# Layer 0's S5 scratch in a pool below the filter's, and the S5 phase doublings on VectorE

## The chip, the cores and the metric

One core of a Trainium2 chip runs the whole program in one launch. The metric is device time in microseconds, the median of several runs. Engines: PE is TensorE (matrix products), DVE is VectorE, ACT is ScalarE, POOL is GpSimd, SP issues the DMA transfers. Each engine works through its own queue in order; semaphores tie the queues together.

## The reference

The model is a two-layer block on 256 latent tokens and 256 context tokens of width 1024. Each layer does the following:

```
h = modulate(rmsnorm(x), shift, scale)      # shift, scale from silu(c) @ ada_w + ada_b
p = h @ w_in                                # columns: Fourier 256, hyena 1152, S5 384
y = concat(fourier(p_f), hyena(p_h, filter), s5(p_s)) @ w_out
x = x + gate * y
x = x + gate_f * ffn(modulate(rmsnorm(x)))  # layer 0: SwiGLU; layer 1: top-2 of 8 experts
```

The hyena filter is a small sine network over 256 positions, windowed, normalised and taken to the frequency domain. It depends on weights only. S5 is a diagonal complex state space, in 24 groups of 16 channels and 64 states, scanned in both directions. Its transition per step is exp(lambda dt), a decay times a phase. The kernel scans over chunks of 8 tokens and turns the states by tables of phases, cos and sin of multiples of the angle, so that the scan itself is real. The multiples come from doublings: squaring a unit complex number and pulling its length back to one.

## The kernel before

The program is written with a tile framework. Tiles are taken from pools, pools lie on two stacks of the on-chip memory (left and right, growing towards each other), and a pool that is closed gives its room to the next one opened on that side. A tile on room that had an owner waits until the owner's pool is released, that is until every access to it has ended. A planner orders each engine's queue at build time from the data dependences, the order in which the program is written (earlier has priority) and its own costs; it also puts waits where memory is reused. So the order on an engine isn't the order of the text.

The start of layer 0, in the order of the text: the pool `filt` (left) holds the filter network `hy_filter` (constants, `hfb`, `hs`, `hd`, `ab`, `rk`, `Kf`). Above it lie `prm` (the S5 parameters, `s5_params`) and `start` (the input `xin`, the norm's scratch, weight tiles). `hy_filter` first runs up to its two sines; then the modulation rows (`ada_pe`), the norm `norm_h` (squares, `rsqrt_small`, then for each of 8 column blocks `nf`, `hH` and `hL`, with `hL` on GpSimd for even blocks and on VectorE for odd ones, L500), then `s5_params`, then the rest of `hy_filter`: for each of two orders the products `pf`, their windowing `hfb` on VectorE, sums `hs` and differences `hd` on GpSimd (L754, L755), and the products `pk`, which become `Kf` and are stored to DRAM (`kd<-Kf`, L772).

`s5_params` computes on 128 x 48 tiles, all on VectorE, up to cos and sin of the angle (`cs`, `sn`). Nine doublings follow (the loop over k), all on GpSimd: `cmul` squares (L241 to L246) from k=1 on, then L360 to L365 normalise. The last six results (`gen`) feed the tables `rotB` and `rotA`, 36 products on GpSimd.

Then `filt` is closed, and `mixers(0, ...)` runs in the pools `z0p` (left, where `filt` was: `uf`, `z0`, `x1`, `x2` and, under one tag, `U` and `ysT`) and `ada0`. On the right it opens `s5p0` (X and the scans' scratch), three matrix buffers `M2`, `M1`, `M0` and, as the last and lowest of that stack, `scr`, the scratch of `s5_mats`. The projection's blocks 11 to 13 are the S5 input: projected (`pacc`), evacuated (`u`, L994), transposed (`pU`, L997), written to `U` (L999), gathered by products into `X` (L1007). `mats(q)` builds the matrices of one sixth of the groups: loads `bs`, `cs` and `d16`, forms `bb`, `bre`, `bim`, writes `M` and clears and fills `rh`, sends `R` to DRAM and reads it back into M (`M<-rd`). `s5_sixth(q)` runs the sixth: products `pv`, two scans on VectorE, the states `Sre`, `Sim`, products `py`. Between sixths, `hy_tile` projects and filters hyena blocks into `z0`, `x1`, `x2`, and `fill0` makes further modulation rows (`ada_ring`). At q=4 `scr` and `M0` are closed and the convolution `conv` of the hyena begins; its products on VectorE use `t_a` (two buffers) and `t_b` (one), each for two of the four products.

After layer 0's mixers come its output projection and feed-forward, with the modulation rows of `ada` (tiles `ar`, `jk` on VectorE, `pd` on GpSimd; the last two in the lasting pool `par`).

Of the kernel before, what the change touches and what calls it, by code (L numbers as in the profile page):

```python
# [8 lines left out]
F32 = mybir.dt.float32  # L9
F32R = mybir.dt.float32r  # L10
I32 = mybir.dt.int32
# [5 lines left out]
D = 1024  # L17
# [5 lines left out]
HY = 384  # L23
S5G = 24
# [109 lines left out]
def build(tc, A, out, dbg=None, upto='all'):  # L134
# [3 lines left out]
    gtt = G.tensor_tensor  # L138
# [109 lines left out]
    def s5_params(p, s5p):  # L248
# [100 lines left out]
        pr, pi = cs, sn  # L349
        t1, t2 = T("gt1"), T("gt2")  # L350
        gen = p.tile([128, 6, 2, 48], F32, name="gen")
        for k in range(9):
            if k >= 3:
                d_re, d_im = gen[:, k - 3, 0], gen[:, k - 3, 1]
            else:
                d_re, d_im = T(f"ph{k}r"), T(f"ph{k}i")
            q_re, q_im = (pr, pi) if k == 0 else (T(f"q{k}r"), T(f"q{k}i"))
            if k:
                cmul(q_re, q_im, pr, pi, pr, pi, t1, t2, G)
            gtt(t1, q_re, q_re, op=mul)  # L360
            gtt(t2, q_im, q_im, op=mul)
            gtt(t1, t1, t2, op=add)
            G.tensor_scalar(t1, t1, -0.5, 1.5, op0=mul, op1=add)
            gtt(d_re, q_re, t1, op=mul)
            gtt(d_im, q_im, t1, op=mul)  # L365
            pr, pi = d_re, d_im
        u, v = (p.tile([128, 48, 4], F32, name=n) for n in ("rtu", "rtv"))
        for tab, k0 in ((rotB, 0), (rotA, 3)):
# [58 lines left out]
    def ada(l, m0, m1, eng, pool):  # L427
        for m in range(m0, m1):
            r = pool.tile([128, D], F32, name="ar", tag="ar", bufs=2)
            SP.dma_start(r, A['adaT'][l, m])  # L430
            for s in range(1 if l == 1 and m >= 16 else 0, 2):
                o = mods[l][:, m, s:s + 1]
                if eng(m, s) == 'v':
                    jk = par.tile([128, D], mybir.dt.bfloat16, name="jk", tag="jk", bufs=1)
                    stt(jk, r, 1.0, crow[:, s], op0=mul, op1=mul, accum_out=o)
                else:
                    pd = par.tile([128, D], F32, name="pd", tag="pd", bufs=1)
                    gtt(pd, r, crow[:, s], op=mul)  # L438
                    act(pd, pd, AF.Copy, accum_out=o)  # L439
            if m % 8 == 7:  # L440
                mods_done(l, m - 7, 8, 1 if l == 1 and m >= 16 else 0)
# [258 lines left out]
    def hy_filter(p, l, kd):  # L700
# [10 lines left out]
                                ap=[[0, 128], [HY, 2], [1, HY]]))  # L711

        def sine(src, b, fr, nm):
            a = p.tile([64, 256], F32, name=nm + "a", tag="sina")
            i = p.tile([64, 256], I32, name=nm + "i", tag="sini")
            nf = p.tile([64, 256], F32, name=nm + "n", tag="sinn")
            o_ = p.tile([64, 256], F32, name=nm + "o", tag="sino", bufs=2)
            ts_(a, src, b, fr, op0=add, op1=mul)
            ts_(i, a, INV2PI, None, op0=mul)
            V.tensor_copy(nf, i)  # L720
            stt(a, nf, -6.28125, a, op0=mul, op1=add)
            stt(a, nf, -1.9350051879882812e-3, a, op0=mul, op1=add)
            stt(a, nf, -3.0199159819567529e-7, a, op0=mul, op1=add)
            ts_(a, a, -3.1415925, 3.1415925, op0=OP.max, op1=OP.min)
            act(o_, a, AF.Sin)
            return o_
# [45 lines left out]
                SP.dma_start(kd[:, o_, f], K)  # L772


    def mixers(l, hH, hL, z2, yH, yL, fill):
        t0 = 0 if l == 0 else 256
        n = 512 - t0
        ns = n // 256
# [76 lines left out]
        def conv(p, K, src0, src1):  # L855
            ce = Kt[1]
            pu = []
            for f in range(4):
                pf = pt_('h' if f < 2 else 'h2', (128, HY), "pU")
                mm(pf, ce[:, f // 2, (f % 2) * 128:(f % 2) * 128 + 128], src0 if f < 2 else src1, True, True)  # L860
                pu.append(pf)
            Yf = p.tile([128, 4, HY], F32, name="Yf", bufs=ns)
            for f in range(2):
                ta, tb, tc_, td = (p.tile([128, HY], F32, name=n_, tag=n_, bufs=b_) for n_, b_ in
                                   (("t_a", 2), ("t_b", 1), ("t_a", 2), ("t_b", 1)))
                tt_(ta, pu[f], K[:, f], op=mul)
                tt_(tb, pu[2 + f], K[:, 2 + f], op=mul)
                gtt(Yf[:, f], ta, tb, op=sub)
                tt_(tc_, pu[f], K[:, 2 + f], op=mul)
                tt_(td, pu[2 + f], K[:, f], op=mul)  # L870
                gtt(Yf[:, 2 + f], tc_, td, op=add)
            return Yf
# [98 lines left out]
        with tc.tile_pool(name=f"s5p{l}", bufs=1, side="right") as p, banks(mat=2, s5=2):  # L971
# [2 lines left out]
            mes, mpool = [ExitStack() for _ in range(nm)], [None] * nm  # L974
            for i in range(nm - 1, -1, -1):
                mpool[i] = mes[i].enter_context(tc.tile_pool(name=f"M{i}_{l}", bufs=1, side="right"))
            SC = ExitStack()
            if l == 0:
                scr = SC.enter_context(tc.tile_pool(name="scr", bufs=1, side="right"))

            U = z2.tile([128, S5G, 4, 16], F32, name="U", tag="ysT")
            raws = {}
            pas = {}
            if l:
# [16 lines left out]
            for q in range(3):  # L1001
# [3 lines left out]
                        mm(px[64 * (1 - par):128 - 64 * par, g], U[:, 8 * q + g].rearrange("p j h -> p (j h)"),  # L1005
                           sel[:, par], True, True)
                act(X[:, 8 * q:8 * q + 8], px, AF.Copy)  # L1007
            ysT = z2.tile([128, 3, n], F32, name="ysT", tag="ysT")
            order = HYO[l]
            done = 0  # L1010

# [19 lines left out]
            for th in range(3):  # L1031
                Y = p.tile([128, 4 if l == 0 else 2, 128], F32, name="Y")
                for h in range(2):
                    q = 2 * th + h
                    if q + nm <= 6 and len(ms) < q + nm:
                        ms.append(mats(q + nm - 1))
                    if l == 0 and q == 4:
                        SC.close()
                        mes[0].close()
                        hA = hes.enter_context(tc.tile_pool(name="hyA0", bufs=1))  # L1040
                        hcon(hA)
                    s5_sixth(p, l, q, *ms[q], X, Y)
                    for _ in range((NHY0, NHY)[l][q]):
                        hy_tile(order[done], raws)
                        done += 1
                    fill(q)
                    if q == (4, 2)[l]:
                        Y0 = [conv(hA, Kt[0], z0[:, s, 0], z0[:, s, 1]) for s in range(ns)]
                    if l and q == 4:
                        zz = hy_second(hp, Y0)  # L1050
                    if l and q == 5:
                        fourier(hp, *fo)
                        hy_last(hp, zz)
                s5_out(l, th, Y, ysT)
# [23 lines left out]
    mdr = [dr.tile([128, 4, 768], F32, name=f"md{q}") for q in range(6)]  # L1078
    rhdr = [dr.tile([128, 4, 64], F32, name=f"rh{q}") for q in range(6)]
    rdr = [dr.tile([32, 4, 240], F32, name=f"rd1{q}") for q in range(6)]  # L1080
    z_es = ExitStack()
    with tc.tile_pool(name="filt", bufs=1) as p_:
        th = tmp.tile([128, KD, 2], F32, name="sth", tag="sth", bufs=1)
        act(th, scol, AF.Tanh, scale=0.5)
# [29 lines left out]
    with z_es:  # L1114
# [3 lines left out]
        with tc.tile_pool(name="z0p", bufs=1) as z2, tc.tile_pool(name="ada0", bufs=1) as p_:  # L1118
            def fill0(q):
                if q == 0:  # L1120
                    ada_ring(4, p_)
                if q == 1:
                    ada_ring(5, p_)
                if q == 3:
                    ada_ring(6, p_)
                if q == 4:
                    ada_ring(7, p_)
            mixers(0, hH, hL, z2, yH, yL, fill0)
        tap('yH0', yH.bitcast(F32))
        tap('yL0', yL.bitcast(F32))  # L1130
        rx_es, xp = ExitStack(), ExitStack()
# [686 lines left out]
```

## Time and profile before

| | |
|---|---|
| median of 3 runs | 1852.7 us (1851.32 to 1853.93) |
| profiled execution | 1846.75 us, of which the span 1844.9 |
| PE busy | 1708.1 us (93%) |
| DVE busy | 824.4 us (45%) |
| ACT busy | 445.1 us (24%) |
| POOL busy | 535.0 us (29%) |
| mean granted PE clock | 0.964 |

The span runs from the first to the last instruction. Busy times of engines overlap, so they don't add up to it. Matrix products are pipelined, and a busy PE isn't PE at its peak. [...] Roughly the second half of the span is layer 1's experts.

### The profile page before, as it was taken

The page shows a single profiled execution, that of the slowest core. Times are in us where ns is not written, and L with a number is a line of the kernel's source. Part 1 is how long each engine was busy: PE and PEld are TensorE (multiplying, and loading weights), DVE is VectorE, ACT ScalarE, POOL GpSimd, SP SyncE. Part 2 cuts the span into 40 slices and gives each one's busy share as a digit, 9 for nine tenths or more (in the row PEclk, how much of TensorE's full clock was granted, in tenths as well). Part 3 has the DMA queues.
Part 4 walks back from the last instruction along what each step waited for, and adds up shares of the span by engine and source line. Part 5 has one row for each costly group of instructions (what it writes and reads, how often), then busy time and mean ns, then how long its engine had stood idle before and what let it go on. Part 6 is the DMA issues. An engine that isn't in the chain of part 4 may idle for free. (4 is left out here: it accounts for less than half of the span.)

```text
span 1844.9 us, 47520 instructions
## 1 busy us (share of the span) xinstructions
PE 1708.1 (93%) x20961; PEld 1195.9 (65%) x20961; DVE 824.4 (45%) x1506; ACT 445.1 (24%) x798; POOL 535.0 (29%) x546
## 2 busy tenths in 40 slices
PE   7988899899989999998898999999999989999984
PEld 3665667777667667778777666666666656666642
DVE  7589968875776767264963001110111101011102
ACT  3332324455444443234332000000000000000000
POOL 5965535567787666012420000000000000000000
PEclk7998999999999999999998999999999999999998
DMA  8243345434556565353839999999999999999993
GB/s 296 88 121 119 100 140 179 142 119 137 175 175 203 188 195 192 120 155 127 248 138 419 405 391 417 419 419 419 419 418 419 419 419 419 415 417 413 415 413 155
DMA packets 150728, 506.83 MB, mean 275 GB/s; under 512 B 18478, under 2 KB 78704, under 8 KB 106480
## 3 DMA queue, kind: packets, MB, share of 16 engines
q1 hardware_dynamic: 150512, 503.70, 71.7%
q8 instruction: 166, 2.72, 0.6%
q14 instruction: 50, 0.41, 0.1%
HBM read 489.34 MB, written 14.32 MB: 273 GB/s over the span
## 5 line engine op out<-in xcount | busy, mean ns | idle before, releaser
L146 PE MATMUL pgu<-raw,xe 128*32 128x256 f32 x9408 | 530.4, 379 | 12.3 <-DMA raw<-in_mwp_dram 11.2
L146 PEld LDWEIGHTS pgu<-raw,xe 128*32 128x32 f32 x9408 | 319.5, 110 | 207.9 <-DMA raw<-in_mwp_dram 15.4
L1639 DVE TENSOR_TENSOR sg<-sg,pgu 128x384 f32<-128x384 f32 (+1 forms) x56 | 28.2, 504 | 630.2 <-ACT sg L1638 630.2
L146 PE MATMUL py<-raw,hT 128*32 128x256 f32 x4704 | 271.5, 379 | 7.8 <-DMA raw<-in_mwp_dram 7.8
L1534 POOL TENSOR_TENSOR ob<-ob,fgb 128x512 f32<-128x512 f32 x1 | 1.3, 1261 | 880.5 <-ACT ob L1533 880.5
L438 POOL TENSOR_TENSOR pd<-ar,crow 128x1024 f32<-128x1024 f32 x88 | 223.7, 2542 | 106.9 <-ACT pd L439 84.9
L190 DVE TENSOR_TENSOR wl<-raw,wh 128x1024 fp32r<-128x1024 f32 x109 | 188.3, 1731 | 92.2 <-ACT wh L189 86.7
L146 PEld LDWEIGHTS py<-raw,hT 128*32 128x32 f32 x4704 | 157.8, 110 | 108.5 <-DMA raw<-in_mwp_dram 7.8
L1638 ACT ACTIVATE sg<-pgu 128x384 f32<-128x384 f32 (+1 forms) x56 | 25.2, 450 | 706.2 <-PE pgu L146 706.2
L189 ACT ACTIVATE wh<-raw 128x1024 fp32r<-128x1024 f32 x109 | 114.5, 1054 | 162.0 <-PE pacc L146 77.9
L146 PE MATMUL pgu<-fhL,wh 128*128 128x512 f32 (+1 forms) x376 | 146.0, 389 | 3.8 <-DVE fhL L541 3.8
L146 PE MATMUL pgu<-fhH,wh 128*128 128x512 f32 (+1 forms) x392 | 146.7, 385 | 1.4 <-ACT sg L1270 0.8
L146 PE MATMUL pgu<-fhH,wl 128*128 128x512 f32 (+1 forms) x360 | 143.0, 398 | 4.0 <-DVE wl L190 3.9
L439 ACT ACTIVATE pd<-pd 128x1024 f32<-128x1024 f32 x88 | 93.1, 1058 | 131.1 <-POOL pd L438 127.7
L146 PE MATMUL pacc<-hL,wh 128*128 128x256 f32 (+1 forms) x248 | 88.2, 357 | 2.9 <-POOL hL L500 2.3
L146 PE MATMUL pacc<-HH,wh 128*128 128x512 f32 (+1 forms) x192 | 76.9, 401 | 14.4 <-DVE xT L1214 11.8
L146 PE MATMUL pacc<-hH,wh 128*128 128x256 f32 (+1 forms) x248 | 86.6, 359 | 3.7 <-DVE hq L829 1.6
L146 PE MATMUL pacc<-hH,wl 128*128 128x256 f32 (+1 forms) x248 | 86.7, 351 | 1.7 <-DVE wl L190 1.7
L146 PEld LDWEIGHTS pgu<-fhL,wh 128*128 128x128 f32 x376 | 72.0, 191 | 21.4 <-DVE fhL L541 4.6
L146 PEld LDWEIGHTS pgu<-fhH,wh 128*128 128x128 f32 x392 | 73.9, 193 | 16.5 <-ACT sg L1270 1.0
L146 PEld LDWEIGHTS pgu<-fhH,wl 128*128 128x128 f32 x360 | 68.7, 191 | 23.8 <-DVE wl L190 5.3
L146 PE MATMUL pacc<-HL,wh 128*128 128x512 f32 (+1 forms) x192 | 74.6, 389 | 0.0
(591 smaller groups left out, 2446.4 us busy)
## 6 DMA issues: line engine op xcount, KB each, us to landing
raw<-in_mwp_dram SPq DMA_DIRECT2D x336, 1024.0 KB
ar<-in_adaT_dram SPq DMA_DIRECT2D x64, 512.0 KB
raw<-in_w_in_dram SPq DMA_DIRECT2D x14, 1024.0 KB
raw<-in_fwg_dram SPq DMA_DIRECT2D x11, 1024.0 KB
raw<-in_fwu_dram SPq DMA_DIRECT2D x11, 1024.0 KB
raw<-in_fwd_dram SPq DMA_DIRECT2D x11, 1024.0 KB
raw<-in_adaN_dram SPq DMA_DIRECT2D x8, 1024.0 KB
ar<-in_adaN_dram SPq DMA_DIRECT2D x16, 512.0 KB
```

The lines of the kernel that those rows point to most:

```text
L146: return PE.matmul(o, l, r, start=start, stop=stop, **kw)
L189: act(h, r, AF.Copy)
L190: tt_(l, r, h.bitcast(F32), op=sub)
L438: gtt(pd, r, crow[:, s], op=mul)
L439: act(pd, pd, AF.Copy, accum_out=o)
L1534: gtt(o_, o_, fgb[:, hs], op=mul)
L1638: act(sg[:, 0:n], p[:, 0:n, 0:128], AF.Silu)
L1639: tt_(sg[:, 0:n], sg[:, 0:n], p[:, 0:n, 128:256], op=mul)
```

## The change

A pool `scr` is opened on the left before `filt`, below it, and closed after layer 0's mixers. It holds what the right-hand `scr` held, and in layer 0 also `U` and `ysT`. `conv` in layer 0 takes its four product tiles from it, under the tags of four tiles of `s5_mats`, one buffer each. To make room, the sine's three tiles share tags with `ab`, `hd` and `hs`, and `jk` and `pd` come from the pool of `ar`. The doublings' instructions go from GpSimd to VectorE; the tables stay on GpSimd.

```diff
@@ s5_params, the loop over k
-                cmul(q_re, q_im, pr, pi, pr, pi, t1, t2, G)
-            gtt(t1, q_re, q_re, op=mul)
-            gtt(t2, q_im, q_im, op=mul)
-            gtt(t1, t1, t2, op=add)
-            G.tensor_scalar(t1, t1, -0.5, 1.5, op0=mul, op1=add)
-            gtt(d_re, q_re, t1, op=mul)
-            gtt(d_im, q_im, t1, op=mul)
+                cmul(q_re, q_im, pr, pi, pr, pi, t1, t2)
+            tt_(t1, q_re, q_re, op=mul)
+            tt_(t2, q_im, q_im, op=mul)
+            tt_(t1, t1, t2, op=add)
+            ts_(t1, t1, -0.5, 1.5, op0=mul, op1=add)
+            tt_(d_re, q_re, t1, op=mul)
+            tt_(d_im, q_im, t1, op=mul)
@@ ada
-                    jk = par.tile([128, D], mybir.dt.bfloat16, name="jk", tag="jk", bufs=1)
+                    jk = pool.tile([128, D], mybir.dt.bfloat16, name="jk", tag="jk", bufs=1)
-                    pd = par.tile([128, D], F32, name="pd", tag="pd", bufs=1)
+                    pd = pool.tile([128, D], F32, name="pd", tag="pd", bufs=1)
@@ hy_filter, sine
-            a = p.tile([64, 256], F32, name=nm + "a", tag="sina")
-            i = p.tile([64, 256], I32, name=nm + "i", tag="sini")
-            nf = p.tile([64, 256], F32, name=nm + "n", tag="sinn")
+            a = p.tile([64, 256], F32, name=nm + "a", tag="ab")
+            i = p.tile([64, 256], I32, name=nm + "i", tag="hd")
+            nf = p.tile([64, 256], F32, name=nm + "n", tag="hs")
@@ mixers, conv
-                ta, tb, tc_, td = (p.tile([128, HY], F32, name=n_, tag=n_, bufs=b_) for n_, b_ in
-                                   (("t_a", 2), ("t_b", 1), ("t_a", 2), ("t_b", 1)))
+                ta, tb, tc_, td = ((scr or p).tile([128, HY], F32, name=n_, tag=g_ if scr else n_, bufs=1 if scr else b_)
+                                   for n_, g_, b_ in (("t_a", "bre", 2), ("t_b", "x2", 1), ("t_a", "bim", 2), ("t_b", "y2", 1)))
@@ mixers
-            SC = ExitStack()
-            if l == 0:
-                scr = SC.enter_context(tc.tile_pool(name="scr", bufs=1, side="right"))
-            U = z2.tile([128, S5G, 4, 16], F32, name="U", tag="ysT")
+            U = (scr or z2).tile([128, S5G, 4, 16], F32, name="U", tag="ysT")
-            ysT = z2.tile([128, 3, n], F32, name="ysT", tag="ysT")
+            ysT = (scr or z2).tile([128, 3, n], F32, name="ysT", tag="ysT")
-                        SC.close()
@@ the program's body
+    scr0 = u_es.enter_context(tc.tile_pool(name="scr", bufs=1))
     with tc.tile_pool(name="filt", bufs=1) as p_:
...
-            mixers(0, hH, hL, z2, yH, yL, fill0)
+            mixers(0, hH, hL, z2, yH, yL, fill0, scr0)
+        u_es.close()
```

## Rows read from the trace of the kernel before

**Rows 1.** Stretches: start:end, length, busy PE, PEld, DVE, ACT, POOL, clock, DMA.
```profile
20.00:57.00 37.00, 33.17 (x137) 17.68 (x138) 29.90 (x81) 16.75 (x31) 33.95 (x93) 0.66 0.68 235
...
57.00:77.00 20.00, 17.66 (x67) 11.86 (x65) 9.44 (x22) 8.72 (x17) 19.75 (x43) 0.91 0.11 41
77.00:97.00 20.00, 20.00 (x100) 15.68 (x100) 8.90 (x13) 6.24 (x10) 17.96 (x32) 1.00 0.37 116
97.00:107.00 10.00, 9.09 (x37) 6.43 (x35) 9.51 (x13) 1.87 (x2) 7.57 (x6) 1.00 0.15 45
107.00:123.00 16.00, 12.16 (x205) 8.33 (x205) 10.62 (x20) 7.35 (x15) 8.74 (x10) 0.79 0.64 207
123.00:150.00 27.00, 23.02 (x219) 15.89 (x218) 26.76 (x58) 8.09 (x15) 15.75 (x18) 1.00 0.55 164
150.00:200.00 50.00, 42.46 (x387) 30.65 (x387) 43.82 (x95) 14.22 (x28) 26.81 (x33) 0.86 0.23 64
200.00:250.00 50.00, 46.21 (x453) 30.29 (x451) 42.68 (x100) 13.86 (x27) 18.15 (x20) 0.93 0.46 150
250.00:276.00 26.00, 25.64 (x92) 15.75 (x91) 17.90 (x31) 8.01 (x15) 12.29 (x13) 1.00 0.36 122
```

**Rows 2.** Timeline of PE: start, duration, instruction, in brackets the idle time before and its releaser.
```profile
61.42 0.50 PE L146 MATMUL pacc<-hL,wh 128*128 128x512 f32 x1 [2.34 <-POOL hL L500]
...
107.68 0.63 PE L582 MATMUL pbt<-ident,bre 128*128 128x128 f32 x4 [1.30 <-DVE Kf L769]
...
112.74 1.13 PE L997 MATMUL pU<-ident,u 128*128 128x128 f32 x4 [2.86 <-ACT U L999]
...
119.71 1.10 PE L146 MATMUL pv<-X,M 128*64 128x64 f32 x32
```

**Rows 3.** Timeline of ACT.
```profile
79.67 0.58 ACT L994 ACTIVATE u<-pacc 128x512 f32<-128x512 f32 x1
...
112.09 1.08 ACT L999 ACTIVATE U<-pU 128x512 f32<-128x512 f32 x2 [3.10 <-DMA kd<-Kf]
```

**Rows 4.** Timeline of SP's queue: the scratch's first load.
```profile
90.47 0.37 SPq L558 DMA_DIRECT2D bs<-in_s5b_dram  x1
```

**Rows 5.** Timeline of POOL, and two groups of its instructions from 18 to 92.
```profile
18.32 1.34 POOL L361 TENSOR_TENSOR gt<-sn 128x48 f32<-128x48 f32 x1 [14.57 <-DVE sn L303]
...
60.10 1.26 POOL L500 TENSOR_TENSOR hL<-nf,hH 128x512 fp32r<-128x512 f32 x1
...
72.16 0.14 POOL L618 MEMSET rh<- 128x4 f32 x2
...
89.85 0.60 POOL L246 TENSOR_TENSOR rotA<-rtu,rtv 128x192 f32<-128x192 f32 x1
...
91.68 0.10 POOL L618 MEMSET rh<- 128x4 f32 x1
...
L362 POOL TENSOR_TENSOR gt<-gt,gt 128x48 f32<-128x48 f32 x9 | 3.1, 347 | 0.6
L363 POOL TENSOR_SCALAR gt<-gt 128x48 f32<-128x48 f32 x9 | 2.4, 269 | 0.7
```

**Rows 6.** Timeline of DVE: dependent and independent neighbours, and a conversion of the norm.
```profile
6.43 1.66 DVE L263 SCALAR_TENSOR_TENSOR dq<-dq,dr 128x48 f32<-128x48 f32 x7
...
14.10 0.18 DVE L294 TENSOR_SCALAR sq<-sy 128x48 f32<-128x48 f32 x1
14.19 0.20 DVE L263 SCALAR_TENSOR_TENSOR aq<-aq,ar 128x48 f32<-128x48 f32 x1
...
40.90 3.67 DVE L447 TENSOR_SCALAR ni<-nv 128x4 int32<-128x4 int32 x1
...
49.10 4.87 DVE L490 TENSOR_TENSOR xin<-xin,pbc 128x512 f32<-128x512 f32 x8 [0.80 <-PE pbc L146]
```

**Rows 7.** Timeline of DVE: the convolution and the first row of modulation.
```profile
245.91 0.56 DVE L870 TENSOR_TENSOR t_b<-pU,K 128x384 f32<-128x384 f32 x1 [1.26 <-POOL Yf L868]
...
292.97 1.82 DVE L435 SCALAR_TENSOR_TENSOR jk<-ar,crow 128x1024 bf16<-128x1024 f32 x1 [0.69 <-DMA ar<-in_adaT_dram]
```

More of the change, by code (lines that the diff above doesn't have):

```diff
@@ L772, in hy_filter, with mixers @@
                 SP.dma_start(kd[:, o_, f], K)
-    def mixers(l, hH, hL, z2, yH, yL, fill):
+    def mixers(l, hH, hL, z2, yH, yL, fill, scr=None):
         t0 = 0 if l == 0 else 256
@@ L1080, in build @@
     rdr = [dr.tile([32, 4, 240], F32, name=f"rd1{q}") for q in range(6)]
-    z_es = ExitStack()
+    z_es, u_es = ExitStack(), ExitStack()
+    scr0 = u_es.enter_context(tc.tile_pool(name="scr", bufs=1))
     with tc.tile_pool(name="filt", bufs=1) as p_:
```

## The prediction

> **What bounds the kernel now.** I read the busy table by stretches first [rows 1]: the reader is to see that the change touches one stage, layer 0 from about 20 to 276 us, and that two engines share it. [...] VectorE has the opposite shape: idle for 22.2 us between 57 and 107 (28 busy of 50), and then full, 113.3 of 127 us from 123 to 250. What VectorE does there is layer 0's S5 (matrices, scans) and the hyena taps. So the stage is first short of inputs and then short of VectorE; work that could start in the idle stretch is waited for in the full one.
>
> The timelines show what it was waiting for. U, the S5 input, cannot be written until the filter has left its memory: the projected columns are evacuated (`u`) at 79.67, but the first write of U runs at 112.09, after an idle wait ended by the DMA that stores the filter [rows 3]. TensorE stands for 2.86 us behind it at 112.74, and the first S5 product (`pv`) comes at 119.71 [rows 2]. The scratch and the first matrix buffer have another gate: the scratch's first load is issued at 90.47 [rows 4], right after the last rotation table ends (89.85 + 0.60), while the `rh` of two matrix buffers was cleared at 72.16 and the third only at 91.68 [rows 5]. The third lies over the parameters' pool, which is released when GpSimd has finished the phases and tables. That chain runs from 18.32 to 90.45, on an engine that is busy 33.95 of 37 us from 20 to 57 and 37.7 of 40 from 57 to 97 [rows 1, 5].
>
> The same engine also holds up the norm: `hL`, which GpSimd makes for every other column block, runs at 60.10 between phase instructions, and TensorE had stood 2.34 us for it [rows 2, 5].
>
> **The change, part by part.** *Phases.* 6 instructions for k=0 and 12 for each of k=1 to 8 are 102; on GpSimd two of their kinds cost 347 and 269 ns on the mean [rows 5], so about 30 us leave it (102 x 0.3). Left are 36 table products and the memsets. On VectorE, 48-element instructions that need each other take 1.66/7 = 0.237 us, independent neighbours start 0.09 apart (14.10, 14.19) [rows 6]: 102 of them cost between 9 and 24 us of VectorE. I take 18, nearer to the dependent row, since in each doubling fewer than half of the instructions have an independent neighbour. VectorE's work from 20 to 57 is 29.90 us [rows 1]; one conversion in it took 3.67 us (40.90, on the norm's chain), where the same operation on 48 columns takes 0.18, beside a GpSimd that ran without a gap [rows 6], and I expect that one back at its size. 29.9 - 3.5 + 18 = 44.4 against 37 us: VectorE is overfilled by about 7 us, which spills past 57 into its 22.2 idle us. The tables then end near 57 + 7 + 3 (the last doubling's products), 25 us or so before 90.45.
>
> [...]
>
> [...]
>
> *Norm.* With GpSimd free, `hL` follows its `hH` at once and the conversion's 3.5 us go; projection starts some 5 us earlier. But TensorE has filter products to do meanwhile, so only its own wait counts: 2.34 us, of which I take 2 (bounds 0 and 4, the second with the slow clock of 57 to 77: 17.66 x 0.09 = 1.6).
>
> *U and the scratch in the lower pool.* U can be written at about 81, not 112.09; the scratch is free from the start, so `bs`, `cs` and the products that need no matrix buffer run early; the first buffer follows the tables, near 67. What is late next is X and the scratch's single copy, then the projections' own pace, and the first `pv` comes at 90 to 95 rather than 119.71. In 107 to 123 TensorE idles 3.84 us and loses 12.16 x 0.21 = 2.6 to the clock: 6.4 in all. U's wait (2.86) and that of 107.68 (1.30) are gone: I take 4 (bounds 0 and 6.4). From 123 to 250 TensorE idles 15.3 us and loses 42.46 x 0.14 + 46.21 x 0.07 = 9.2 to the clock. VectorE can take 22.2 - 7 = 15 us of this work forward; a list of several interlocked chains doesn't recover all of it, and TensorE can't win more than its idle time: half, 7 (bounds 0 and 24.5).
>
> *Costed at nothing.* The convolution's four scratch tiles in their own buffers remove a wait like the 1.26 us at 245.91 [rows 7], but TensorE is busy 25.64 of 26 us from 250 to 276 [rows 1], which hides it; without that cover it is worth 2. `jk` and `pd` move to the pool of `ar`; the first `jk` waits for the load of `ar` anyway (292.97) [rows 7]; if they came later than it, up to 2 lost. The sine's three tiles share tags with tiles written after them. Loads of `bs`, `cs` and `d` can now pass onto SP's queue ahead of the norm's input: three issues of 0.37 to 0.9 us, so at most 2 us lost there. The kernel's order is made by a planner, and all of this shifts every queue after it; I give that nothing, with 3 us either way.
>
> Sum: 2 + 4 + 7 = 13 us off the profiled execution's 1846.75 (span 1844.9 and 1.85 around it), 1833.75. The median of the runs shown is 1852.7, 5.95 above that execution; what is timed later compares with the median, so I forecast 1852.7 - 13 = 1839.7, rounded to 1840. Within 0.2% is 3.7 us, about what a measurement of this kernel can tell from no change.
>
> **Rivals.**
> *Better overlap.* VectorE takes its 15 us forward and TensorE's clock stays up because its short gaps are gone: 4 + 6.4 + 15 = 25 us, 1827. For it: the slow rows (0.79, 0.86) follow waits. Against: from 123 on VectorE has work of later sixths that nothing moves. The lowest clock is that of 107 to 123, the stretch with the two waits.
>
> *The filter still gates.* Columns of the hyena part (`x2`, `z0`, `x1`, `uf`) stay in the pool that opens where the filter was. If the filter's store ends as late as now, the two accumulators hold hyena columns until 112 whatever S5 does, and TensorE gets only 2 to 4 us back: 1849. For it: U's releaser at 112.09 is just that store. Against: the filter's chain is itself held by GpSimd, which the phases leave.
>
> *VectorE becomes the bound of the start (slower).* The phases stand ahead of the filter's second half in program order and among the norm's instructions. At 24 us, VectorE has 26.4 + 24 = 50 us of work for the 37 from 20 to 57, 13 over. If that stands before the norm's `xin` and the filter's products rather than after them, projection starts later by 13 - 5 (the norm's gain above) = 8 us, TensorE idles for it, and the later gain falls to 4: 4 us slower, 1857. It decides from the point where more than 9 us of phases precede the norm. Against: norm instructions come first in program order, and dependent phases leave gaps that others fill.
>
> **How the numbers follow.** Forecast 0.53 (1834 to 1846 by itself), better overlap 0.16, filter still gates 0.17, VectorE at the start 0.14. Range: low 1825 (the better overlap with 2 to spare), high 1853 (the gated case with its 3 us of order and a little); outside lie most of the slower case and a tail below. Faster by over 0.2% means under 1849: forecast and better overlap, and a third of the gated case, 0.74; same: the rest of the gated case and a little of the slower one, 0.13; slower 0.13.
>
> **What would show it.** Right: phases on VectorE between 20 and 65; last `rotA` before 70; U written within 2 us of its transpose, near 81 to 90; first `pv` by 95; VectorE's busy share from 57 to 107 well over 28 of 50; TensorE's idle time from 57 to 250 down by 8 us or more, and everything after 276 merely moved. Wrong: VectorE's `xin` products later than 49.1, TensorE waiting longer before its first projection than 2.34; U early but `pv` still near 119, by X, the matrix buffer or the accumulators; or a gain at 250 that has gone by 400.

## The result, and the profile after

The changed kernel takes 1873.2 us (1873.0 to 1874.3, four runs) beside 1852.9 for the kernel before: 1.011 of it, interval 1.0096 to 1.0123, 20 us slower. The forecast was 1840, 13 us faster, in a range of 1825 to 1853. The profiled executions are further apart, 1874.25 and 1846.75, in part because the profiled one of before lies under its median.

Where the time went is read off four marks in the traces, in us from the span's start: the first product of the projection, the first sixth's R sent to DRAM, the hyena's `zs` at the end of the S5 stage, and the first `HH`, the hidden layer of layer 0's feed-forward as ScalarE writes it. (Two expectations below call this last mark the first matmul on HH; the first product that reads HH comes 70 us later.) The other kernels of this table are the experiments below, each set against the runs of before timed with it, whose medians were 1850.1 to 1852.9.

| kernel | first projection | first R stored | `zs` | first `HH` | median, ratio to before |
|---|---|---|---|---|---|
| before | 57.9 | 117.0 | 262.7 | 384.9 | 1 |
| the change | 68.4 | 126.7 | 280.5 | 406.0 | 1873.2, 1.0110 |
| doublings alone | 64.6 | 123.7 | 266.5 | 389.8 | 1858.9, 1.0053 |
| pools alone | 56.4 | 116.6 | 270.6 | 396.3 | 1866.1, 1.0080 |
| U and ysT alone | 58.3 | 121.2 | 264.3 | 386.3 | 1858.7, 1.0051 |
| change, tables on VectorE | 65.0 | 112.1 | 265.8 | 390.8 | 1860.3, 1.0057 |
| change, doublings behind norm | 64.7 | 127.2 | 279.6 | 404.1 | 1863.8, 1.0070 |
| pools alone, convolution late | 59.0 | 116.5 | 264.7 | 390.0 | 1858.5, 1.0056 |

So the change is 10.5 us late at the first projection, 9.7 when the first R is stored, 8.3 at the sixth and last R (238.0 against 229.6), and 17.8 at `zs`: from the last R to `zs` it takes 42.5 us, not 33.1. The stretches of the kernel after, as in [rows 1]:

```profile
20.00:57.00 37.00, 33.41 (x133) 17.89 (x134) 36.45 (x146) 15.15 (x28) 17.83 (x25) 0.59 0.71 241
57.00:77.00 20.00, 13.05 (x42) 9.12 (x42) 19.76 (x49) 7.46 (x14) 11.38 (x17) 0.69 0.06 21
77.00:97.00 20.00, 14.49 (x61) 9.44 (x59) 15.98 (x23) 8.52 (x14) 17.00 (x28) 0.99 0.05 20
97.00:107.00 10.00, 9.36 (x28) 7.28 (x29) 3.08 (x5) 0.00 (x0) 3.10 (x4) 0.50 0.66 210
107.00:123.00 16.00, 16.00 (x97) 12.49 (x95) 4.67 (x6) 4.87 (x8) 2.98 (x2) 0.89 0.14 50
123.00:150.00 27.00, 20.39 (x318) 14.05 (x319) 24.00 (x50) 7.30 (x16) 11.61 (x13) 0.81 0.43 138
150.00:200.00 50.00, 38.90 (x360) 27.10 (x356) 45.97 (x92) 15.45 (x31) 32.60 (x36) 0.90 0.41 116
200.00:250.00 50.00, 44.21 (x399) 30.62 (x399) 42.09 (x93) 15.72 (x28) 21.71 (x25) 1.00 0.38 118
```

VectorE (third figure) is now full from 20 to 77: 56.2 of 57 us, against 39.3. GpSimd (fifth) lost about what it should: 71.7 us of work from 20 to 97 became 46.2. TensorE (first) idles 36.6 of the 193 us from 57 to 250, against 22.4.

What VectorE did ahead of the norm's `xin` products is plain in its timeline, with GpSimd's below it (start, duration, instruction, idle before):

```profile
49.53 0.15 DVE L461 SCALAR_TENSOR_TENSOR ny<-nt,ny 128x4 f32<-128x4 f32 x1
...
53.05 1.22 DVE L190 TENSOR_TENSOR wl<-raw,wh 128x1024 fp32r<-128x1024 f32 x1
...
55.01 0.58 DVE L241 TENSOR_TENSOR gt<-gen 128x48 f32<-128x48 f32 x1
55.52 0.57 DVE L242 TENSOR_TENSOR gt<-gen 128x48 f32<-128x48 f32 x1
56.12 0.63 DVE L243 TENSOR_TENSOR q6r<-gt,gt 128x48 f32<-128x48 f32 x1
...
58.55 0.21 DVE L360 TENSOR_TENSOR gt<-q6r 128x48 f32<-128x48 f32 x1
...
61.26 1.27 DVE L490 TENSOR_TENSOR xin<-xin,pbc 128x512 f32<-128x512 f32 x2
...
81.24 0.20 DVE L365 TENSOR_TENSOR gen<-q8i,gt 128x48 f32<-128x48 f32 x1
```
```profile
55.00 0.53 POOL L241 TENSOR_TENSOR rtu<-rotB,gen 128x192 f32<-128x192 f32 x1 [2.29 <-DVE gen L365]
55.49 0.53 POOL L242 TENSOR_TENSOR rtv<-rotB,gen 128x192 f32<-128x192 f32 x1
56.10 0.59 POOL L243 TENSOR_TENSOR rotB<-rtu,rtv 128x192 f32<-128x192 f32 x1
```

The norm's last statistic is there at 49.7, but the end of one doubling, two whole ones, the start of a fourth and two `wl` stand before `xin` in the queue, so it starts at 61.26 and not at 49.10 [rows 6]. The doublings of k=6 run in step with GpSimd's table products, 0.57 to 0.63 us each; the same kind of instruction takes 0.21 at 58.55, where GpSimd rests. The last doubling ends at 81.4. The durations of the 102 instructions add up to 34.1 us (31.4 with overlaps counted once), where the forecast took 18.

Then TensorE's waits, and what stood behind the longest (the second fence is a view of one tile: count, then shortest, median and longest in ns, first and last start):

```profile
67.11 1.65 PE L146 MATMUL prk<-ident,rc 128*128 128x128 f32 x6 [6.95 <-DVE mods L382]
68.41 1.20 PE L146 MATMUL pacc<-hH,wh 128*128 128x512 f32 x2
...
97.64 0.80 PE L146 MATMUL pacc<-hH,wl 128*128 128x512 f32 x1 [6.14 <-DVE wl L190]
98.23 0.63 PE L146 MATMUL pacc<-hH,wh 128*128 128x512 f32 x1
...
125.92 1.15 PE L146 MATMUL pv<-X,M 128*64 128x64 f32 x32
```
```profile
L190 DVE TENSOR_TENSOR wl<-raw,wh x2: 1212/5457/9702, 87.9 to 97.5; 128x1024 fp32r<-128x1024 f32 x2
```
```profile
89.02 0.58 POOL L246 TENSOR_TENSOR rotA<-rtu,rtv 128x192 f32<-128x192 f32 x1
89.57 0.99 POOL L754 TENSOR_TENSOR hs<-hfb 128x384 f32<-128x384 f32 x1
...
95.30 1.20 POOL L615 TENSOR_TENSOR M<-rotA,rotB 128x256 f32<-128x256 f32 x2
96.44 0.10 POOL L618 MEMSET rh<- 128x4 f32 x1
```

One `wl` took 9.70 us, where 1.21 is plain, while GpSimd ran 14 instructions without a gap; it ended 1.04 us after the last of them. TensorE stood 6.14 us for it, and the products after it take 0.63, not the 0.40 they take from 110.5 on: the granted clock is 0.50, half of full speed, in the stretch 97 to 107, and 1.00 from 110.5 to 112.3. The tables end at 89.6, as late as before (90.45). The lines of U and of the scratch that answer [rows 3, 4], on ScalarE's and SP's queues:

```profile
91.06 0.60 ACT L997 ACTIVATE U<-pU 128x512 f32<-128x512 f32 x1 [0.71 <-PE pU L995]
108.71 0.60 ACT L997 ACTIVATE U<-pU 128x512 f32<-128x512 f32 x1 [17.05 <-PE pU L995]
120.61 0.60 ACT L997 ACTIVATE U<-pU 128x512 f32<-128x512 f32 x1 [0.70 <-PE pU L995]
```
```profile
16.21 0.39 SPq L558 DMA_DIRECT2D bs<-in_s5b_dram  x1
```

The store of the filter no longer holds U, and the scratch loads at 16. But U's first part comes at 91.06, ten us behind the forecast, its third waits for its transposed projection until 120.61, and `pv` comes at 125.92, not 119.71.

### The profile page after: what moved, and what is told of

The parts are those of the page before. It is cut to its first block, busy times and chain, and to the rows that moved or that the text cites. A ratio compares the mean times of both kernels' runs of the same rounds, so it can differ in the third digit from the quotient of the medians.

```text
span 1872.3 us, 47517 instructions
## 1 busy us (share of the span) xinstructions
PE 1717.5 (92%) x20961; PEld 1199.1 (64%) x20961; DVE 846.7 (45%) x1608; ACT 445.3 (24%) x798; POOL 510.3 (27%) x444
## 5 line engine op out<-in xcount | busy, mean ns | idle before, releaser
L190 DVE TENSOR_TENSOR wl<-raw,wh 128x1024 fp32r<-128x1024 f32 x109 | 196.6, 1807 | 99.7 <-ACT wh L189 93.0
L439 ACT ACTIVATE pd<-pd 128x1024 f32<-128x1024 f32 x88 | 93.1, 1058 | 128.2 <-POOL pd L438 127.2
L146 PE MATMUL pacc<-HH,wh 128*128 128x512 f32 (+1 forms) x192 | 78.0, 407 | 15.9 <-DVE xT L1214 12.2
L146 PEld LDWEIGHTS pgu<-fhL,wh 128*128 128x128 f32 x376 | 71.7, 191 | 21.6 <-DVE fhL L541 5.4
L146 PEld LDWEIGHTS pgu<-fhH,wl 128*128 128x128 f32 x360 | 68.0, 189 | 22.4 <-DVE wl L190 4.1
L146 PE MATMUL pacc<-HH,wl 128*128 128x512 f32 (+1 forms) x192 | 74.0, 392 | 1.5 <-DVE wl L190 1.4
```

Source lines behind the costliest of these rows:

```text
L146: return PE.matmul(o, l, r, start=start, stop=stop, **kw)
L190: tt_(l, r, h.bitcast(F32), op=sub)
```

## The experiments

**Each part alone.** The first kernel is the one before with the doublings' diff and nothing else. The second is the change with the doublings back on GpSimd.

> The kernel before with the doublings on VectorE and nothing else of the change. Theory A (the doublings are the loss: they stand in VectorE's queue before the norm's xin products): xin later than 49.1 by 8 us or more, the first projection later than 57.9, 10 to 20 us slower. Theory B (the pool is the loss: S5 work let in early fills VectorE and GpSimd before the norm and the filter): within 4 us of before, xin near 49.

> The whole change, but the doublings stay on GpSimd. Theory A: no slower than before, 0 to 13 us faster, since U and the scratch come early. Theory B: 10 to 20 us slower than before, with early bre and bim products on VectorE before xin.

Measured: 1858.9, 8.6 us slower than before (ratio interval 1.0037 to 1.007), and 1866.1, 15.9 slower (1.0053 to 1.0106). Both parts cost, and their sum, 24.5, is near the change's 20. The doublings alone delay `xin` to 57.4 and the first projection and the first R by 6.7 us each: theory A by its marks, though the time is under its 10 to 20. The pools alone delay neither, with `xin` at 49.9, so theory B has the time right but not the reason. They lose their time at the stage's end: last sixth's `Y` at 261.2 against 251.2, though its R is stored earlier (226.7 against 229.6). The moves of `jk`, `pd` and the sine's tags were not run apart from the pools. The stretch from `zs` to the first `HH` takes 124.5 to 125.7 us in the seven kernels with the whole pool part and 122.0 to 123.3 in the four without, so some 2 us are lost there too, by a cause that stays open.

The third is the kernel before with U and ysT alone in a low pool `up`; `scr` stays on the right.

```diff
-            U = z2.tile([128, S5G, 4, 16], F32, name="U", tag="ysT")
+            U = (up or z2).tile([128, S5G, 4, 16], F32, name="U", tag="ysT")
...
-            ysT = z2.tile([128, 3, n], F32, name="ysT", tag="ysT")
+            ysT = (up or z2).tile([128, 3, n], F32, name="ysT", tag="ysT")
...
```

> The kernel before with U and ysT alone in a pool below the filter's; the scratch of the matrices stays where it was and the doublings on GpSimd. Theory A and B both: U no longer waits for the filter's store (112.09 before), written near 85; 0 to 6 us faster. If it is slower by more than 4 us, moving U is itself a loss, by another order of the queues.

Measured: 1858.7 (1.0031 to 1.0071), 8.4 slower, so by the rule set beforehand moving U is itself a loss. U is written at 82.2 and X at 100.8, 30 and 15 us earlier than before, and the first R is stored at 121.2, 4 later. U was not what the stage waited for. But `zs` is only 1.6 late and the first `HH` 1.4: the other 7 of the 8.4 us lie behind it and are not explained. The six sixths' R follow one another at some 22 us on the mean (before: 117, 137, 160, 187, 210, 230), and each sixth needs its matrices.

**Contention.** The change, with the 36 table products on VectorE too, so that GpSimd has no products beside the doublings:

```diff
-                     u[:, :, 0:n], v[:, :, 0:n], G)
+                     u[:, :, 0:n], v[:, :, 0:n])
```

> The whole change, and the 36 table products on VectorE as well, so that GpSimd has no short products between 46 and 90. If VectorE's doublings are slow because GpSimd's table products run beside them (0.4 to 0.6 us each in step with GpSimd's, against 0.2 alone), they are 0.2 us each here, xin comes before 58 and the time is 3 to 10 us below the change's 1873. If the load of VectorE is what counts, xin is no earlier than 61.26 and the time 1873 or more.

Measured: 1860.3 (1.0041 to 1.0074), 10 slower than before but about 10 less than the change by the ratios. `xin` starts at 57.8, the doublings of k=4 to 6 (read in the kernel below that has the late convolution besides) take 0.2 us an instruction where the change's took up to 0.63, and the two `wl` at 87.53 take 3.21 us together, not 10.84. The first R is stored at 112.1, earlier than before. Putting more work on the full engine made it faster, which contention and the missing 9.7 us `wl` fit and VectorE's load alone does not. The first R does not decide the stage, though: here the last one, too, is stored 8.2 us earlier than before (221.4 against 229.6), and `zs` comes 3.1 later.

**The order of VectorE's queue.** The change, with the doublings from k=4 on queued behind the last of the eight `xin` products (`XIN[7]`):

```diff
         for k in range(9):
+          with (tc.issue_after(XIN[7].ins) if k >= 4 else nullcontext()):
...
```

> The change, with the doublings from k = 4 on (six instructions of a complex product and six of the rescaling each) queued on VectorE behind the last of the norm's eight xin products; nothing else differs. In the changed kernel the norm's rsqrt ended at 49.7 us and its broadcast stood at 52.45, but VectorE worked through q5, q6 and two wl until 61.26 before the first xin product. Theory A (the order of VectorE's queue made the norm late): first xin product at 50 to 53, first projection product at 58 to 61 instead of 68.4, and 7 to 10 us off the end: about 1865 us. Theory B (the matrices' chain sets the stage, and the doublings put later only delay the tables on GpSimd): xin as early as under A, but the last rotA at 92 or later, the first request that stores a sixth's R at 126 or later, and the time unchanged, 1871 to 1876.

Measured: 1863.8 (1.0053 to 1.0086). `xin` starts at 51.45, as theory A says, but the first projection only at 64.7: the norm's other input is late next, the modulation rows, whose products stand in TensorE's queue behind filter products that run at a granted clock of 0.50 (from 46 to 64.7, where before shows 0.84 from 46 to 57).

```profile
51.45 4.87 DVE L493 TENSOR_TENSOR xin<-xin,pbc 128x512 f32<-128x512 f32 x8 [1.03 <-PE pbc L146]
...
63.82 0.17 DVE L383 TENSOR_TENSOR mods<-mods,colp 128x8 f32<-128x8 f32 x1 [4.20 <-ACT mods L406]
```

The tables then run to 102 and the first R is stored at 127.2: theory B in the stage, while the time is theory A's. The 7 us that its ratio lies under the change's are not found in the traces, which differ by 2 us at the first `HH`; its profiled execution, 1870.5, was the longest of its four.

**The convolution at the stage's end.** The pools alone, with one number changed, so that the convolution is asked for in the last sixth:

```diff
-                    if q == (4, 2)[l]:
+                    if q == (5, 2)[l]:
```

> The pool part alone (doublings on GpSimd), with the filter convolution of layer 0 asked for in the last sixth instead of the fifth (one line). With the pool part alone VectorE's scan of the last sixth and its Y came 10 us later than before (245.2 and 261.2 against 235.8 and 251.2) though the sixth's matrices were as early, and its time was 1866.1. Theory A (the convolution, whose products no longer wait for their own buffers, stands ahead of the last sixth in VectorE's and TensorE's queues): last Y back at about 251 to 254, zs at 262 to 265 instead of 270.6, time 1857 to 1860. Theory B (the convolution only moves behind the last sixth, and the filter's path takes over as the end of the stage): last Y earlier, but zs still at 269 to 274 and the time 1864 to 1870.

Measured: 1858.5 (1.004 to 1.0073), 7.6 under the pools alone: theory A by `zs` and the time. What had let the convolution go ahead shows in its filter's load and its first product, against the last sixth's scan. SP and VectorE, before:

```profile
235.21 0.50 SPq L852 DMA_DIRECT2D K<-kd  x1
...
235.84 0.69 DVE L655 TENSOR_TENSOR_SCAN w<-rh,w 128x256 f32<-128x256 f32 x1
242.80 0.56 DVE L866 TENSOR_TENSOR t_a<-pU,K 128x384 f32<-128x384 f32 x1 [0.34 <-PE pU L146]
```

The pools alone:

```profile
210.90 0.35 SPq L852 DMA_DIRECT2D K<-kd  x1
...
227.35 0.55 DVE L868 TENSOR_TENSOR t_b<-pU,K 128x384 f32<-128x384 f32 x1
245.17 1.50 DVE L655 TENSOR_TENSOR_SCAN w<-rh,w 128x256 f32<-128x256 f32 x1
```

The filter is loaded 24 us earlier. Before, the convolution's pool took the room of `scr` and `M0`, and `scr` was in use up to the last R (229.6); with `scr` on the left at most `M0` stands in its way. In the seven kernels with the whole pool part the load is issued at 207 to 222, in the four without at 235 to 243, U alone among them (235.7). The runs don't separate this from the convolution's own four tiles.

With the late convolution `Y` came back only to 258.3, 2.9 of the 5.8 us that `zs` won. In this trace TensorE runs a hyena projection from 226.98 to 233.7 ahead of most of the fifth sixth's `py` products, which so come at 234.63, though the states were ready at 229.8; before, they came at 230.18 and the projection behind them. The last sixth's first product on VectorE is 4.7 us late by then (238.18 against 233.51), of the 7.1 that `Y` is late. The rest of what `zs` won is TensorE's clock: in the pools alone it stood 3.28 us for `Y`, and its next products took 7.37 us (clock 0.68 from 261.7 to 270.9); here it stood 0.28, and they took 5.33 (1.00 from 258.7 to 265). Pools alone first:

```profile
261.68 2.08 PE L146 MATMUL pyT<-ident,Y 128*128 128x128 f32 x8 [3.28 <-DVE Y L688]
263.54 7.37 PE L146 MATMUL pi<-Yf,ci 128*128 128x384 f32 x16
```
```profile
258.75 1.16 PE L146 MATMUL pyT<-ident,Y 128*128 128x128 f32 x8 [0.28 <-DVE Y L688]
259.74 5.33 PE L146 MATMUL pi<-Yf,ci 128*128 128x384 f32 x16
```

**Mended together.** Tables on VectorE and the late convolution; those two and the doublings behind the norm; and the layout of before with doublings and tables on VectorE, behind the norm.

> The change with two edits: the 36 table products on VectorE too, and the filter convolution asked for in the last sixth. Of all kernels so far the one with the tables alone stored its first R earliest (112.1 us) and was at 1860.3; the convolution in the last sixth took 7.6 us off the pool part alone (zs 270.6 to 264.7). Theory A (the two losses add, each of its own place): zs at 258 to 261 instead of 265.8, time 1850 to 1854, the kernel before at best. Theory B (the stage's end is set by another queue once the convolution is away): zs at 264 to 267, time 1857 to 1862.

> The change with three edits together: the 36 table products on VectorE too, the doublings from k = 4 on behind the norm's xin products, the convolution in the last sixth. The change with the tables alone on VectorE was 1860.3. Theory A (each of the three losses is of its own place): first xin product at 50 to 53, first projection at 57 to 60, first R stored by 113, zs at 255 to 258, time 1843 to 1849, below the kernel before. Theory B (the chain of the six sixths' matrices at some 22 us each sets the stage, so that an earlier norm gives nothing): first projection as early, first R at 112 to 118, zs at 262 to 268, time 1853 to 1861.

> The kernel before with its own buffers (no change of pools), doublings and table products all on VectorE, the doublings from k = 4 on behind the norm's xin products. The doublings alone on VectorE were 1858.9, with the first projection at 64.6 and the first R stored at 123.7. Theory A (what the doublings cost was their place ahead of the norm and VectorE's and GpSimd's products slowing one another): first projection at 57 to 59, last rotA at 75 or earlier, first R at 105 to 112, time 1842 to 1849. Theory B (VectorE is simply full between 57 and 107 us, where the projections need its wl and hL): last rotA at 85 or later, first R at 117 or later, time 1853 to 1860.

Measured: 1860.6 (1.0033 to 1.0076), `zs` 266.7; 1859.2 (1.0029 to 1.0064), `zs` 264.3; 1871.6 (1.0089 to 1.013), `zs` 279.1. Theory B each time, the last one worse than either theory. The mends do not add, and none brings back the time of before. In the last kernel VectorE is busy 35.1 of the 36 us from 57 to 93, where the tables end, and its first R comes at 125.6; the second kernel, with the same tables in the same order and the scratch in the low pool, had it at 117.9. What starts U does not decide. What does is only in part the matrices: from the last R to `zs` the three take 46.0, 37.9 and 40.7 us, and why the first and the third are so long was not followed.

**Is one profile enough?**

> The kernel before once more, unchanged, for a second profile. The first profile (span 1844.9) was 6 us under the median of its runs, and its part from the first FFN matmul on HH (384.9) to the last output (1837.3) was 1452.4 us, against 1458.1 in the changed kernel, 1456.8 to 1462.5 in three others and 1452.5 in one. If that spread is from one execution to the next: this profile's span is 1846 to 1852 with the same 384 to 386 at the first matmul on HH, and the part behind it is 1454 to 1459. If it is the kernels' own: 1452 to 1453 again.

> The changed kernel once more, unchanged, for a second profile. What was put down to the start and the mixer of layer 0 should stand again: first xin product at 61 to 62 us, first R stored at 126 to 127, zs at 280 to 281, first FFN matmul on HH at 405 to 407; the part behind that is free to lie between 1452 and 1460. If the marks before 300 us move by more than 1 us from one execution to the next, the reading of the single profile falls.

Measured: spans 1845.2 and 1877.5. The marks stand within 0.6 us up to the first `HH` (before 384.4, change 406.1). Behind it the kernel before took 1453.1 us (1452.4 in the first profile), the change 1463.2 (1458.1). That part varies by 5 us in the change's own executions, and two of each don't show whether the change loses there as well. The 21 us up to `HH` are what is explained here, and the timed runs, 20 us apart, leave little beside them.

**The two engines by themselves.**

> Nothing of the reference is computed; the output is filled from the last tile. Eleven stages of the disputed cost by itself, on tiles in SBUF: 24 VectorE products of 128x48 alone and beside 44 GpSimd products of 128x192; 6 of 128x1024 alone and beside the same; 24 one-input 128x48 tensor_scalar alone and beside; 12 products of 128x512 with one input in PSUM alone and beside; 24 products of 128x48 beside GpSimd tensor_scalar of 128x192, beside 80 GpSimd products of 128x48, and beside 40 ScalarE copies of 128x512. Theory A (the two engines share their way into SBUF, and hold each other up): two-input VectorE products alone 0.20 and 1.2 us, beside GpSimd each waits for about a GpSimd instruction, 0.55 to 0.65 for 128x48 and 2 us or more for 128x1024, and nothing of that beside ScalarE. Theory B (VectorE is slowed only by its own queue and semaphores): 0.20 and 1.2 in every stage.

Groups of instructions (busy, mean ns of one): four pairs, alone and then beside GpSimd products; then two-input products beside one-input GpSimd work (`v8o`) and beside ScalarE copies (`v10o`).

```profile
L166 DVE TENSOR_TENSOR v0o<-xs,one 128x48 f32<-128x48 f32 x24 | 5.0, 208 | 5.3 <-DMA xs<-in_xT_dram 4.6
L166 DVE TENSOR_TENSOR v1o<-r,one 128x48 f32<-128x48 f32 x24 | 14.6, 608 | 0.8
L166 DVE TENSOR_TENSOR v2o<-r,one 128x1024 f32<-128x1024 f32 x6 | 7.3, 1225 | 0.2
L166 DVE TENSOR_TENSOR v3o<-r,one 128x1024 f32<-128x1024 f32 x6 | 8.7, 1450 | 0.2
...
L168 DVE TENSOR_SCALAR v4o<-r 128x48 f32<-128x48 f32 x24 | 4.5, 188 | 0.8
L168 DVE TENSOR_SCALAR v5o<-r 128x48 f32<-128x48 f32 x24 | 7.7, 322 | 0.8
...
L170 DVE TENSOR_TENSOR v6o<-r,pb 128x512 f32<-128x512 f32 x12 | 8.2, 687 | 0.5
L170 DVE TENSOR_TENSOR v7o<-r,pb 128x512 f32<-128x512 f32 x12 | 8.2, 687 | 0.4
...
L166 DVE TENSOR_TENSOR v8o<-r,one 128x48 f32<-128x48 f32 x24 | 5.6, 234 | 0.8
...
L166 DVE TENSOR_TENSOR v10o<-r,one 128x48 f32<-128x48 f32 x24 | 5.0, 208 | 0.8
```

Theory A, but for the long products, which it put at 2 us or more. A VectorE product of 0.21 us lasts 0.61, about one GpSimd product (0.59), when both have two inputs in SBUF; long ones take 1.45, not 1.23, and slow GpSimd (710 ns on the mean, not the 589 beside the short ones). Nothing is paid with one input in PSUM (687 both times) or beside ScalarE (208), and little beside one-input GpSimd work (234). For short products the price here is to last as long as one GpSimd instruction; what the two engines share, the rows don't show.

**The wait of 9.7 us** is not explained by that. Three more runs looked for it: GpSimd without gaps between its instructions, GpSimd with the kernel's own operands, and VectorE coming in the middle of the stream.

> Nothing of the reference is computed; the output is filled from the last tile. In the stages measured before, GpSimd wrote one tile over and over, its instructions started 0.66 us apart at 0.59 us each, and VectorE's two-input products came in between them, one for each. In the changed kernel GpSimd's products from 81.28 to 96.5 us write different tiles and start before the one ahead has ended (87.36 0.52, 87.85), and there two VectorE products took 10.84 us. Here GpSimd's 44 products of 128x192 write four tiles in turn. Theory A (without a gap VectorE is not let in at all): the first two-input VectorE product beside them takes some 23 us, until GpSimd's last has ended (44 times 0.52 to 0.56), the one-input tensor_scalar too, the product with one input in PSUM stays at 0.69, and beside 12 GpSimd products the wait is 6 to 7 us. Theory B (the gap does not matter): one VectorE product per GpSimd instruction as before, 0.6 us each, and the wait in the changed kernel was of another cause.

> Nothing of the reference is computed; the output is filled from the last tile. Stages as before, but GpSimd's stream has the operands of the kernel: stage 0, 26 products of 128x192 with one operand spread along the last axis (the tables' shape) beside 4 VectorE products of 128x1024; stage 1, 16 products of 128x512 with both operands spread (the matrices' shape); stage 2, 16 sums of 128x384 (the filter's); stage 3, the three mixed in pairs; stage 4, the same mix beside 4 one-input instructions on 128x4; stage 5, the same mix beside 16 products of 128x48. Theory A (spread or mixed operands let GpSimd keep VectorE out over several instructions): in at least one stage the longest VectorE product is above 4 us, its plain 1.22 and the length of several GpSimd instructions. Theory B (each hand-over comes at the end of one GpSimd instruction, whatever the operands): none above 2.4 us for 128x1024 and none above 1.3 us for 128x48; then the 9.7 us of the changed kernel stay open.

> Nothing of the reference is computed; the output is filled from the last tile. The stages of the run with the kernel's operands, except that VectorE comes late: its instructions wait for the last of 8 ScalarE copies (about 5 us), so that GpSimd is in the middle of its stream when the first one asks. Stage 0: 4 VectorE products of 128x512 started together with GpSimd's 16 sums of 128x384; stage 1 the same, late; stage 2 late, beside 16 products of 128x512; stage 3 late, 4 one-input instructions on 128x4; stage 4 late, 16 products of 128x48 beside a mix; stage 5 late, one product. Theory A (who comes while a gapless stream runs is kept out of it): the first late instruction takes 5 us or more in stages 1 to 3, as the one of 9.7 us in the changed kernel. Theory B (one hand-over per GpSimd instruction): none above 2.2 us, and that one stays open.

Theory B in all three. Without gaps products of 128x48 took 0.50 on the mean; with the kernel's operands the longest of 128x1024 took 1.96 and of 128x48 0.98; coming late, the longest of 128x512 took 1.59. The longest ones, by tile:

```profile
L190 DVE TENSOR_TENSOR v1o<-r,one x4: 1218/1726/1961, 39.1 to 43.8; 128x1024 f32<-128x1024 f32 x4
```
```profile
L194 DVE TENSOR_TENSOR v5o<-c,one x1: 1587/1587/1587, 117.8 to 117.8; 128x512 f32<-128x512 f32 x1
```

Yet the two `wl` with the 9.70 took 10.84 us together again in the second profile of the change, and the 3.67 of before [rows 6] stood as 4.01 in its second one. In the first profiles the two lie over 14 and 10 GpSimd instructions, nearly all overlapping the next by some 0.03 us. That a VectorE instruction can last as long as such a stream is seen; that the stream shuts it out is likely but not shown, and why it happens in the kernels and not in these runs stays open.

## Why the prediction was wrong

*Phases.* The step that failed is the one that put the overfill behind the norm: "VectorE is overfilled by about 7 us, which spills past 57 into its 22.2 idle us". It did spill, to 77, but the queue had doublings and early S5 products ahead of `xin`, so what moved back was the norm, and the tables ended at 89.6, not at 67. The term of 18 us was mis-sized too: it took 34.1. Where GpSimd rests a doubling's instruction takes 0.18 to 0.21 us, which would make 21; those that met GpSimd's instructions took up to three times as long (0.63), ten still more (0.80 to 1.32). That the two engines lengthen each other's instructions never entered the sum, though the conversion's 3.67 us beside a GpSimd without a gap [rows 6] stood in the text.

*Norm.* 2 us gained were forecast; the first projection came 10.5 later and the first R 9.7. That the one delay simply became the other is not shown: with the tables on VectorE too the projection was 7.0 late and the first R 4.9 early, and in the change the wait for the long `wl` and the slow clock behind it cost some 12.4 us in between (6.14 and, by estimate, 6.3). At the norm it is the mechanism of the rival called slower, which I priced at 8 us there and 4 in the end, and gave 0.14.

*U and the scratch.* The filter's store and the old scratch no longer held them (first U 91, scratch 16), and it was worth nothing: U and ysT alone brought X forward by 15 us and the stage not at all. "What is late next is X and the scratch's single copy" named the wrong wait: with X 15 us early the first R was 4 us late. That "the first buffer follows the tables, near 67" failed by the tables' 89.6; and the tables alone don't set the first R either, for with the doublings alone they ended at 82.1, 8.4 us earlier than before, and the first R came 6.7 later. So neither the 4 nor the 7 us of this step came.

*Costed at nothing.* The convolution. I priced its tiles by the wait of 1.26 us that they end, and overlooked that its filter can be loaded some 24 us earlier once `scr` is away. Its products went ahead of the last sixth in both queues, and 7.6 us were lost, 5.8 of them seen at `zs`. What remains of the last sixth's delay with the convolution behind it has a hyena projection in TensorE's queue ahead of it; putting that back was not tried.

Of the signs named for it, only VectorE's busy share from 57 to 107 (38.8 of 50) and, within a microsecond, U's time came true. Two of those named against it, `xin` later than 49.1 and a wait of more than 2.34 us before the first projection (6.95), came true as well.

## What to carry to other kernels

An engine's busy share says how much work fits, not where it will stand: before moving work to an emptier engine, name what on its queue is on the critical path during the same microseconds, here the norm, and tie the moved work behind it. Short VectorE work with both inputs in SBUF lasted about one GpSimd instruction apiece beside GpSimd products (0.61 us, not 0.21), so split dependent stages between these two engines only where they don't run together. An early input is worth what the latest input of the same step allows. And when memory is moved, ask who waited for its old place: what is freed there can overtake the work that counts.

## What the runs showed of the hardware

With the two engines by themselves, VectorE products with one operand in PSUM took 687 ns alone and beside GpSimd's, which stayed at 589; products of 208 ns stayed so beside ScalarE copies. A one-input VectorE instruction, 188 ns alone, took 322 beside GpSimd products. And TensorE's clock was low behind three waits. After 3.28 us of waiting the granted clock was 0.68 from 261.7 to 270.9 in the pools alone, and two groups of products took 9.45 us where they took 6.49 at 1.00 behind the short wait. After 6.14 us it was 0.50 from 97.6 to 110.2 in the changed kernel, 12.6 us, of which about half, 6.3, are lost by an estimate from the clocks 0.50 and 1.00. In both places the wait was paid about a second time, but that is no fixed price: after the 6.95 us of waiting that ended at 67.11 the clock was 0.51 for 5.9 us, some 2.9 lost by the same estimate, and 1.00 from 73 to 80.
